# The low parts of all weights on one engine: GpSimd's share of the weight split is given to VectorE

## The chip, the cores and the metric

The kernel runs on one core of one Trainium2 chip. The core has TensorE (PE in the profile), VectorE (DVE), ScalarE (ACT), GpSimd (POOL) and SyncE (SP), which issues the weight transfers. Each engine works through its own queue in order and waits for the others by semaphores. The metric is the device time of one execution in microseconds (us); less is better. Several executions are timed, and their median is given.

## What is computed

Two stacks of transformer layers follow each other on 512 tokens of width 1024, all in float32. Cut to what matters:

```
# first stack, twice:
x = x + 0.5 * rmsnorm(swiglu(rmsnorm(x), w_gate, w_up, w_down))    # ffn1, hidden width 2816
x = x + rmsnorm(token_mixing(rmsnorm(x)))                          # mix1: band, difference and stick-breaking attention
x = x + 0.5 * rmsnorm(swiglu(rmsnorm(x), ...))                     # ffn2
# 16 meta tokens are put in front; second stack, twice:
h = h + rmsnorm(mixer(rmsnorm(h)))                                 # mix2: forgetting attention, a conv of 31 taps, a short conv
h = h + rmsnorm(down(silu(conv3(g)) * conv3(up)))                  # ffn3
```

Every product with a weight, `y @ w`, is computed to about float32 from operands of a reduced format (float32r). A float32 operand is split into a high part, which is its rounding to that format, and a low part, which is what is left. Then `x w` is formed as `xh wh + xl wh + xh wl`, three matmuls for each one of the mathematics.

## The kernel before

**Tiling.** The state lies as eight tiles of 128 channels by 528 tokens (`xT`). Tokens are worked in two halves, of up to 272 columns. A weight comes in units of 128 by up to 1056 values: eight blocks of 128 by 128 side by side. A unit is used by one run of matmuls (`mm3`, lines 222 to 224, or lines 799 to 801 for the value projections).

**The weight stream.** `plan` lists all units in the order of use. `load` (line 183) brings one unit in two pieces: SyncE issues the transfer of a piece into a raw buffer `wr` (four of them), ScalarE rounds it into `wh` (line 200), and the subtraction `wl = wr - wh` follows (line 201). `wh` and `wl` have four buffers each. `wunit` hands out the next unit and calls for those up to three ahead. Which engine does the subtraction is chosen at line 193. Before, it is GpSimd for all units of the mixers (mix1 and mix2) and for the first four units of each block but the first (`HEADS`), and VectorE for all others. A unit has two pieces, so that GpSimd does 292 of the 1068 subtractions: 128 in mix1, 124 in mix2, 40 at the heads of the feed-forward blocks.

**What else VectorE does.** At the boundary between two blocks (`boundary`, line 374 on) it scales the block's result by its norm (line 383), adds it to the state (line 389), forms the low part `xl` of the next operand (line 405), and sums squares (lines 346 and 426). In mix1 it does the running products of the stick-breaking part (lines 991 and 993), softmax parts, low parts of the weights of attention (line 927), and it takes the outputs from the PSUM bank (lines 939, 940, 965). In mix2 it computes two depthwise convolutions of 31 taps (line 1350, 120 instructions in the program), evacuates the projections, and forms the forget gate `lf` (line 1186), which TensorE transposes (line 1211).

**The order.** The program is written as generators that are woven together by estimated step times (`weave`, `pipeline`, `Filler`). Behind that stands a scheduler of the framework, which orders the instructions of each engine by its own estimate of when their operands are there. So a change of one instruction's engine can move others, on all engines.

Below, a "subtraction" is always an instruction of line 201, a "tap" one of line 1350.

Of the kernel before, what the change touches and what calls it, by code (L numbers as in the profile page):

```python
# [79 lines left out]
def block_stack_kernel(ctx: ExitStack, tc: tile.TileContext, x_in, meta_in, vec_in, lam_in, wup1, wdn1, wqk1,  # L80
# [3 lines left out]
    act, dve, pe, pool = nc.scalar, nc.vector, nc.tensor, nc.gpsimd  # L84
# [53 lines left out]
    plan, ready, HEADS = [], {}, set()  # L138
# [26 lines left out]
    def wsrc(key, n, c0):  # L165
        kind, l, name = key[:3]
        if name in ("up", "dn"):
            arr = {"up": (wup1, wup2), "dn": (wdn1, wdn2)}[name][kind == "ffn3"]
            i = l if kind == "ffn3" else 2 * l + (kind == "ffn2")
            return arr[i, key[3], key[4]] if name == "up" else arr[i, key[3], :, c0:c0 + n]  # L170
        arr = {"mix1": {"qk": wqk1, "v": wv1, "wo": wo1},
               "mix2": {"qk": wqk2, "v": wv2, "wo": wo2, "cv": wcv2, "pw": wpw2}}[kind][name]
        ap = arr[l]
        for i in key[3:]:
            ap = ap[i]
        return ap[:, 0:n]
# [8 lines left out]
    def load():  # L185

        i = head[1]
        head[1] += 1
        k, n, c0 = plan[i]
        hi = wp.tile([128, 1056], F32R, tag="wh", bufs=4, name="wh")  # L190
        lo = wp.tile([128, 1056], F32R, tag="wl", bufs=4, name="wl")
        ready[i] = hi, lo
        eng = pool if k[0][:3] == "mix" or i in HEADS else dve
        src = wsrc(k, n, c0)
        m = n // 2 if n == 1056 else (n // 128 + 1) // 2 * 128
        for a, b in ((0, m), (m, n)):
            raw = wp.tile([128, 528], F32, tag="wr", bufs=RAWS, name="wr")
            nc.sync.dma_start(out=raw[:, :b - a], in_=src[:, a:b])
            yield raw
            act.activation(out=hi[:, a:b], in_=raw[:, :b - a], func=ACTF.Copy)  # L200
            eng.tensor_tensor(out=lo[:, a:b], in0=raw[:, :b - a], in1=hi[:, a:b].bitcast(F32), op=ALU.subtract)  # L201

    def fetch(to):
        while head[1] < min(to, len(plan)):
            for _ in load():
                pass
# [37 lines left out]
    class Whole:  # L244

        i, n, g, c = None, TALL - T0, slice(T0, TALL), slice(0, TALL - T0)
# [1378 lines left out]
    g0 = VCOL[pre[k0], l0]  # L1625
    nc.sync.dma_start(out=vec[:, g0:g0 + KC], in_=vec_in[:, g0:g0 + KC])
    u0, u1 = load(), load()
    load_x(0, 0, 2)
    next(u0)
# [170 lines left out]
```

## Time and profile before

| | us |
|---|---|
| timed runs | 3595.52, 3599.58, 3600.26 |
| median | 3599.58 |
| profiled execution | 3593.15 |
| its span, first to last instruction | 3591.3 |
| mean granted TensorE clock | 0.966 of full speed |

The profiled execution lies 6.4 us under the median, and 1.85 us of it lie around the span. The page of the profile gives busy time for each engine, the same in 40 slices, and the costliest groups of instructions. Busy time on TensorE is modelled, since its matmuls overlap. The blocks follow each other in the span about so: ffn1 to 370, mix1 to 683, ffn2 to 1062, ffn1 to 1441, mix1 to 1755, ffn2 to 2134, mix2 to 2458, ffn3 to 2859, mix2 to about 3190, ffn3 to the end. So there are nine boundaries between blocks and two passes through each mixer.

### The profile page before, as it was taken

Reading aid. Unit: us, or ns where it says so; the run is one execution under the profiler, and the core shown is the slowest. Engines: PE = TensorE matmul, PEld = TensorE weight load, DVE = VectorE, ACT = ScalarE, POOL = GpSimd, SP = SyncE. Lnnn points to the kernel's source line nnn. Section 1 sums busy time; section 2 is a strip of 40 time slices with the busy share of each in tenths; the row PEclk is TensorE's granted clock in tenths of the full one; section 3 lists DMA queues with packets and bytes.
Section 4 is the critical chain, followed back from the end, with each engine's and each line's share of the span. In section 5 each row is a group of like instructions: output and inputs, shape, how many; then the busy total and the mean of one; then the engine's idle time right before and its main releaser. Section 6 shows DMA issues by size and latency. Waiting matters only on the chain.

```text
span 3591.3 us, 56445 instructions
## 1 busy us (share of the span) xinstructions
PE 3443.0 (96%) x21851; PEld 3055.9 (85%) x21851; DVE 2025.5 (56%) x4145; ACT 1530.7 (43%) x3335; POOL 439.4 (12%) x439
## 2 busy tenths in 40 slices
PE   9999989999999999989999998989999989899998
PEld 8888877888888888877988888879999988799998
DVE  5442777654335442777644349546774386467753
ACT  5323555533234332555633334555443345554432
POOL 0000322200010000322200014212000132120000
PEclk9999999999999999999999999979999989899999
DMA  4233212132332223222133322102222221023232
GB/s 143 94 94 94 71 56 73 49 106 94 94 91 92 94 90 93 66 61 70 60 100 94 93 90 78 51 30 71 95 94 88 87 75 57 30 62 104 90 92 78
DMA packets 165820, 291.43 MB, mean 81 GB/s; under 512 B 19456, under 2 KB 36896, under 8 KB 165552
## 3 DMA queue, kind: packets, MB, share of 16 engines
q1 hardware_dynamic: 163648, 287.13, 25.7%
q8 instruction: 172, 2.82, 0.3%
q10 hardware_dynamic: 1904, 0.70, 0.1%
q14 instruction: 96, 0.79, 0.1%
HBM read 285.62 MB, written 2.13 MB: 80 GB/s over the span
## 4 chain that ended last, share of the span: by engine, by line
PE 83%; DVE 13%; ACT 2%; issue 1%; DMA 0%; POOLq 0%; SPq 0%; ACTq 0%; DVEq 0%
PE ps_acc L222 9%; PE ps_acc L223 9%; PE ps_acc L224 9%; PE ps_s L222 7%; PE ps_s L223 7%; PE ps_s L224 7%; PE ps_x L223 4%; PE ps_x L222 4%; PE ps_x L224 4%; PE ps_o L222 4%; PE ps_o L223 4%; PE ps_o L224 4%; DVE y L1350 3%; PE ps_o L840 2%; PE ps_s L823 2%
## 5 line engine op out<-in xcount | busy, mean ns | idle before, releaser
L200 ACT ACTIVATE wh<-wr 128x512 fp32r<-128x512 f32 (+2 forms) x1068 | 615.4, 614 | 1105.3 <-PE ps_acc L223 453.5
L201 DVE TENSOR_TENSOR wl<-wr,wh 128x512 fp32r<-128x512 f32 (+1 forms) x776 | 499.3, 670 | 440.6 <-ACT wh L200 429.9
L201 POOL TENSOR_TENSOR wl<-wr,wh 128x512 fp32r<-128x512 f32 (+1 forms) x292 | 408.5, 1421 | 2627.5 <-ACT wh L200 2619.8
L222 PE MATMUL ps_acc<-xh,wh 128*128 128x256 f32 (+2 forms) x1600 | 537.7, 336 | 0.0
L223 PE MATMUL ps_acc<-xl,wh 128*128 128x256 f32 (+2 forms) x1600 | 526.9, 329 | 0.0
L224 PE MATMUL ps_acc<-xh,wl 128*128 128x256 f32 (+2 forms) x1600 | 525.4, 328 | 0.0
L223 PE MATMUL ps_s<-xl,wh 128*128 128x512 f32 (+3 forms) x1088 | 361.5, 332 | 12.8 <-DVE xl L405 12.5
L222 PE MATMUL ps_s<-xh,wh 128*128 128x512 f32 (+3 forms) x1088 | 360.8, 332 | 1.0 <-ACT xh L312 0.7
L224 PE MATMUL ps_s<-xh,wl 128*128 128x512 f32 (+3 forms) x1088 | 359.7, 331 | 0.2 <-DVE wl L201 0.2
L222 PEld LDWEIGHTS ps_acc<-xh,wh 128*128 128x128 f32 x1600 | 311.4, 195 | 28.3 <-issue 2.2
L224 PEld LDWEIGHTS ps_acc<-xh,wl 128*128 128x128 f32 x1600 | 310.6, 194 | 25.0 <-issue 0.2
L223 PEld LDWEIGHTS ps_acc<-xl,wh 128*128 128x128 f32 x1600 | 311.3, 195 | 22.4
L223 PEld LDWEIGHTS ps_s<-xl,wh 128*128 128x128 f32 x1088 | 207.5, 191 | 34.7 <-DVE xl L405 15.1
L222 PEld LDWEIGHTS ps_s<-xh,wh 128*128 128x128 f32 x1088 | 207.9, 191 | 21.8 <-ACT xh L312 1.1
L224 PEld LDWEIGHTS ps_s<-xh,wl 128*128 128x128 f32 x1088 | 207.4, 191 | 19.7 <-DVE wl L201 0.4
L222 PE MATMUL ps_x<-xh,wh 128*128 128x256 f32 (+3 forms) x608 | 206.1, 339 | 0.0
L223 PE MATMUL ps_x<-xl,wh 128*128 128x256 f32 (+3 forms) x608 | 203.9, 335 | 0.0
L224 PE MATMUL ps_x<-xh,wl 128*128 128x256 f32 (+3 forms) x608 | 203.0, 334 | 0.0
L223 PE MATMUL ps_o<-xl,wh 128*128 128x512 f32 (+3 forms) x544 | 179.7, 330 | 5.1 <-DVE xl L405 5.1
L222 PE MATMUL ps_o<-xh,wh 128*128 128x512 f32 (+3 forms) x544 | 179.0, 329 | 0.0
L224 PE MATMUL ps_o<-xh,wl 128*128 128x512 f32 (+3 forms) x544 | 178.7, 328 | 0.0
L223 PE MATMUL ps_acc<-hl,wh 128*128 128x256 f32 (+1 forms) x528 | 168.7, 319 | 0.0
(360 smaller groups left out, 7982.6 us busy)
## 6 DMA issues: line engine op xcount, KB each, us to landing
wr<-in_wup_dram SPq DMA_DIRECT2D x528, 256.0 KB, 2.8
wr<-in_wdn_dram SPq DMA_DIRECT2D x192, 256.0 KB, 2.7
wr<-in_wqk_dram SPq DMA_DIRECT2D x96, 256.0 KB, 2.7
wr<-in_wdn_dram SPq DMA_DIRECT2D x96, 192.0 KB, 2.6
wr<-in_wo_dram SPq DMA_DIRECT2D x64, 256.0 KB, 2.7
wr<-in_wv_dram SPq DMA_DIRECT2D x40, 256.0 KB, 2.6
wr<-in_wcv_dram SPq DMA_DIRECT2D x40, 256.0 KB, 2.6
dec<-fdram SPq DMA_DIRECT2D x16, 264.0 KB, 3.7
```

What stands on the lines that cost most here:

```text
L200: act.activation(out=hi[:, a:b], in_=raw[:, :b - a], func=ACTF.Copy)
L201: eng.tensor_tensor(out=lo[:, a:b], in0=raw[:, :b - a], in1=hi[:, a:b].bitcast(F32), op=ALU.subtract)
L222: pe.matmul(out=o, lhsT=wh[wsl], rhs=xh[xsl], start=start, stop=False)
L223: pe.matmul(out=o, lhsT=wh[wsl], rhs=xl[xsl], start=False, stop=False)
L224: pe.matmul(out=o, lhsT=wl[wsl], rhs=xh[xsl], start=False, stop=stop)
L823: pe.matmul(out=o, lhsT=a[R, qs], rhs=b[R, ks], start=j == 0, stop=j == 2 and mask is None)
L840: pe.matmul(out=o[:, q0:], lhsT=v, rhs=p[j], start=kb == 0 and j == 0, stop=kb == n - 1 and j == 1)
L1350: dve.scalar_tensor_tensor(out=y[:, s:], in0=t[0][:, :TALL - s], scalar=w[:, 30 - s:31 - s], in1=y[:, s:], op0=ALU.mult, op1=ALU.add))
```

## The change

One line of `load` is changed. The subtraction of every piece of every weight is issued on VectorE.

```diff
@@ load(), line 193 @@
-        eng = pool if k[0][:3] == "mix" or i in HEADS else dve
+        eng = dve
```

Nothing else is changed in the source. GpSimd keeps some 150 small instructions (constants, the scaling of `lrow`, half of the last block's additions). The scheduler orders the rest anew from there.

At the boundary from ffn1 to mix1 (span 370 to 390) VectorE's queue held no subtraction before. `xT` is the state, `f` the block's result, `xl` the low part of the next operand. Before:

```order
L358 RECIPROCAL rt<-rt_s 128x2
L360 COPY R<-rt 128x256
L346 TENSOR_TENSOR sqo<-sqo 128x256
L383 TENSOR_TENSOR f<-f,ps_t 128x256 x2
L389 TENSOR_TENSOR xT<-xT,f 128x256
L383 TENSOR_TENSOR f<-f,ps_t 128x256
L389 TENSOR_TENSOR xT<-xT,f 128x256
L383 TENSOR_TENSOR f<-f,ps_t 128x256
L405 SCALAR_TENSOR_TENSOR xl<-xT,vec,xh 128x256
```

After, at the same place:

```order
L358 RECIPROCAL rt<-rt_s 128x2
L360 COPY R<-rt 128x256
L201 TENSOR_TENSOR wl<-wr,wh 128x512
L346 TENSOR_TENSOR sqo<-sqo 128x256
L383 TENSOR_TENSOR f<-f,ps_t 128x256
L201 TENSOR_TENSOR wl<-wr,wh 128x512
L383 TENSOR_TENSOR f<-f,ps_t 128x256
L389 TENSOR_TENSOR xT<-xT,f 128x256
L383 TENSOR_TENSOR f<-f,ps_t 128x256
L389 TENSOR_TENSOR xT<-xT,f 128x256
L383 TENSOR_TENSOR f<-f,ps_t 128x256
L405 SCALAR_TENSOR_TENSOR xl<-xT,vec,xh 128x256
```

Two subtractions stand in the run, four more come before the last of the eight `xl`, and two behind it.

In mix2 the forget gate `lf` (line 1186) stands between taps in VectorE's queue. Before, the rows ahead of it were:

```order
L1350 SCALAR_TENSOR_TENSOR y<-av,vec,y 128x506
L771 SCALAR_TENSOR_TENSOR ql<-qt,qh 128x256
L1350 SCALAR_TENSOR_TENSOR y<-av,vec,y 128x505
L1350 SCALAR_TENSOR_TENSOR y<-av,vec,y 128x527
L1350 SCALAR_TENSOR_TENSOR y<-av,vec,y 128x504
L769 TENSOR_TENSOR qt<-ps_acc,rb 128x272
L1350 SCALAR_TENSOR_TENSOR y<-av,vec,y 128x503
L771 SCALAR_TENSOR_TENSOR ql<-qt,qh 128x272
L1350 SCALAR_TENSOR_TENSOR y<-av,vec,y 128x502
L1350 SCALAR_TENSOR_TENSOR y<-av,vec,y 128x526
L1350 SCALAR_TENSOR_TENSOR y<-av,vec,y 128x501
L1186 SCALAR_TENSOR_TENSOR lf<-lft,lfe 128x40
```

After:

```order
L201 TENSOR_TENSOR wl<-wr,wh 128x512
L1350 SCALAR_TENSOR_TENSOR y<-av,vec,y 128x511
L201 TENSOR_TENSOR wl<-wr,wh 128x512
L1350 SCALAR_TENSOR_TENSOR y<-av,vec,y 128x510
L1346 TENSOR_SCALAR y<-av,vec 128x528
L1350 SCALAR_TENSOR_TENSOR y<-av,vec,y 128x509
L1350 SCALAR_TENSOR_TENSOR y<-av,vec,y 128x527
L1350 SCALAR_TENSOR_TENSOR y<-av,vec,y 128x508
L769 TENSOR_TENSOR qt<-ps_acc,rb 128x272
L1350 SCALAR_TENSOR_TENSOR y<-av,vec,y 128x507
L771 SCALAR_TENSOR_TENSOR ql<-qt,qh 128x272
```

Three taps follow these rows, and then line 1186. Between the first evacuation of the block (line 1338) and line 1186 there were 29 taps and no subtraction; now there are 25 taps and six subtractions (three more stand ahead of that first evacuation, around line 360).

On TensorE the transposes of that gate (line 1211) stood in the middle of the key projection of the first pair of heads. Before:

```order
L222 MATMUL ps_acc<-xh,wh 128x272
L223 MATMUL ps_acc<-xl,wh 128x272
L224 MATMUL ps_acc<-xh,wl 128x272
L1211 MATMUL ps_t<-ident,lf 8x16
L1211 MATMUL ps_t<-ident,lf 8x128 x4
L222 MATMUL ps_acc<-xh,wh 128x272
```

After:

```order
L224 MATMUL ps_acc<-xh,wl 128x256
L823 MATMUL ps_s<-qh 16x16
L823 MATMUL ps_s<-ql,qh 16x16
L823 MATMUL ps_s<-qh,ql 16x16
L827 LDWEIGHTS identb
L827 MATMUL ps_s<-fmask,identb 16x16
L823 MATMUL ps_s<-qh 128x144
L1211 MATMUL ps_t<-ident,lf 8x16
L1211 MATMUL ps_t<-ident,lf 8x128 x4
```

Between the value projection and line 1211 there were 37 triples of lines 222 to 224; now there are 48 triples and the first score products. In the second mix2 it is the same on both engines, with a few more score products.

## Rows read from the trace of the kernel before

**Rows 1.** The page, busy us of each engine, its share and instructions.

```profile
PE 3443.0 (96%) x21851; PEld 3055.9 (85%) x21851; DVE 2025.5 (56%) x4145; ACT 1530.7 (43%) x3335; POOL 439.4 (12%) x439
```

**Rows 2.** Groups by line: busy us, mean ns | idle before, and what ended it.

```profile
L201 DVE TENSOR_TENSOR wl<-wr,wh 128x512 fp32r<-128x512 f32 (+1 forms) x776 | 499.3, 670 | 440.6 <-ACT wh L200 429.9 <-PE ps_s L224 0.2
L201 POOL TENSOR_TENSOR wl<-wr,wh 128x512 fp32r<-128x512 f32 (+1 forms) x292 | 408.5, 1421 | 2627.5 <-ACT wh L200 2619.8 <-DVE f L383 4.3 <-POOL wl L201 1.7
```

**Rows 3.** Stretches: length; busy PE, PEld, DVE, ACT, POOL; PEclk, DMA share, GB/s.

```profile
352.00:412.00 60.00, 53.10 (x422) 52.21 (x422) 40.20 (x86) 28.08 (x68) 16.93 (x12) 0.94 0.21 67
412.00:500.00 88.00, 77.62 (x519) 65.41 (x518) 67.91 (x114) 48.81 (x119) 28.64 (x20) 0.96 0.22 67
500.00:660.00 160.00, 151.25 (x947) 124.38 (x947) 111.60 (x333) 87.63 (x234) 33.66 (x25) 0.94 0.18 55
...
2165.00:2265.00 100.00, 87.16 (x707) 81.21 (x707) 89.84 (x175) 43.83 (x108) 41.12 (x49) 0.95 0.26 80
2265.00:2450.00 185.00, 172.99 (x1165) 149.97 (x1164) 82.08 (x237) 100.84 (x247) 45.66 (x68) 0.87 0.15 45
```

**Rows 4.** The same stretches for line 201 alone: DVE, then POOL busy.

```profile
2165.00:2265.00 100.00, 0.00 (x0) 36.02 (x24) 0.95 0.26 80
2265.00:2450.00 185.00, 0.00 (x0) 39.24 (x30) 0.87 0.15 45
```

**Rows 5.** VectorE's groups by form, and by line for the taps of line 1350.

```profile
L201 DVE TENSOR_TENSOR wl<-wr,wh 128x512 fp32r<-128x512 f32 x680 | 454.0, 687 | 440.6 <-ACT wh L200 429.9 <-PE ps_s L224 0.2
L389 DVE TENSOR_TENSOR xT<-xT,f 128x256 f32<-128x256 f32 x120 | 67.5, 563 | 0.0
L346 DVE TENSOR_TENSOR sqo<-sqo 128x256 f32<-128x256 f32 x119 | 65.8, 567 | 107.0 <-ACT sqo L338 106.5
...
L771 DVE SCALAR_TENSOR_TENSOR ql<-qt,qh 128x256 fp32r<-128x256 f32 x32 | 23.3, 737 | 3.0 <-ACT qh L770 3.0
...
L549 DVE TENSOR_TENSOR hl<-gu,hh 128x256 fp32r<-128x256 f32 x16 | 6.7, 421 | 0.2
...
L568 DVE SCALAR_TENSOR_TENSOR y<-z,vec,y 128x526 f32<-128x526 f32 (+3 forms) x176 | 132.2, 757 | 3.2 <-ACT y L566 0.5
L1350 DVE SCALAR_TENSOR_TENSOR y<-av,vec,y 128x525 f32<-128x525 f32 (+16 forms) x120 | 108.1, 907 | 0.8
```

**Rows 6.** First boundary, in order of time: start, us, engine, line, tiles [idle before].

```profile
374.71 0.41 DVE L389 TENSOR_TENSOR xT<-xT,f 128x256 f32<-128x256 f32 x1
375.78 1.52 DVE L389 TENSOR_TENSOR xT<-xT,f 128x256 f32<-128x256 f32 x1
375.61 2.85 POOL L201 TENSOR_TENSOR wl<-wr,wh 128x512 fp32r<-128x512 f32 x2 [1.43 <-ACT wh L200]
```

**Rows 7.** TensorE's waits, whole span: us in total, times, longest.

```profile
PE ps_o L840 <- DVE yl L940: 24.7, 12, 3.3
PE ps_t L354 <- DVE sqo L346: 24.5, 10, 4.8
PE ps_t L1211 <- DVE lf L1186: 21.4, 2, 10.7
PE ps_s L223 <- DVE xl L405: 12.5, 11, 2.2
PE ps_o L223 <- DVE xl L405: 5.1, 6, 1.5
```

**Rows 8.** First mix2, in order of time: VectorE, GpSimd and TensorE up to line 1211.

```profile
2172.61 0.42 DVE L1338 TENSOR_TENSOR av<-ps_s,rb 128x256 f32<-128x256 f32 x1 [1.01 <-ACT rb L300]
2209.94 4.07 DVE L1350 SCALAR_TENSOR_TENSOR y<-av,vec,y 128x502 f32<-128x502 f32 x3
2213.93 0.19 DVE L1186 SCALAR_TENSOR_TENSOR lf<-lft,lfe 128x40 f32<-128x40 f32 x1
...
2210.07 3.40 POOL L201 TENSOR_TENSOR wl<-wr,wh 128x512 fp32r<-128x512 f32 x2 [3.68 <-ACT wh L200]
...
2203.22 0.29 PE L224 MATMUL ps_acc<-xh,wl 128*128 128x272 f32 x1
2214.17 1.13 PE L1211 MATMUL ps_t<-ident,lf 16*8 16x16 f32 x5 [10.66 <-DVE lf L1186]
```

## What the change was predicted to do

> **What bounds the kernel now.** The page comes first: TensorE is busy for 96% of the span and VectorE for 56%, so TensorE's own work sets most of the time [rows 1]. What an engine beside it can win or lose lies in the 148 us in which TensorE is not busy (3591.3 - 3443.0). The second view is therefore the list of what TensorE waits for: the longest items are all VectorE's, 24.7 us for line 940, 24.5 for 346, 21.4 for 1186, and 12.5 and 5.1 for `xl` [rows 7]. The third is the table by stretch, which says where VectorE is full: 40.2 of 60 us at a boundary, 67.9 of 88 and 111.6 of 160 in the middle of mix1, 89.8 of 100 in the stretch of mix2 that holds the taps, 82.1 of 185 in the rest of mix2 [rows 3]. GpSimd delays TensorE nowhere in the list. So the question is what 292 more instructions do to VectorE just where TensorE waits for it.
>
> **The price of a subtraction.** On GpSimd one takes 1421 ns on average [rows 2]. On VectorE the same 128x512 form takes 687 ns [rows 5]. 292 x 0.687 = 201 us of new work on VectorE.
>
> **What is refunded.** VectorE is slowed while GpSimd subtracts. At the first boundary the addition of line 389 takes 0.41 us at one place and 1.52 us at another, where a pair of GpSimd's subtractions runs [rows 6]. The means show how common that is. An instruction of two 128x256 operands from SBUF takes 421 ns where GpSimd is idle (line 549), but lines 389, 346 and 771 average 563, 567 and 737 [rows 5]: 120 x 0.142 + 119 x 0.146 + 32 x 0.316 = 44.5 us. The taps average 907 ns against 757 for the like instruction of line 568: 120 x 0.15 = 18 us [rows 5]. Taken in this way for every VectorE instruction that overlaps one of GpSimd's (585 of them, of which 190 are slowed by over 0.1 us; line 389 in rows 6 is one), the loss is 152 us. It goes away with GpSimd's subtractions. The load of VectorE thus rises by 201 - 152 = 49 us only, in a kernel in which it idles for 1566.
>
> The Trainium skill ("SBUF — State Buffer", Who interferes with whom) gives the mechanism: a VectorE instruction with two SBUF inputs and a GpSimd instruction that reads SBUF need the same port, and the second of them waits for the whole of the first. The 0.41 and 1.52 us agree. By that rule nothing of the loss stays once GpSimd computes no low part.
>
> **Boundaries, nine of them.** In the first one VectorE runs without a pause from 371.7 to 386.7 us, and TensorE waits for `xl` there. Between those times the refund, instruction by instruction, is 5.8 us (16 that overlap GpSimd, the first a line 346, the 1.52 us of rows 6 among them). Six subtractions now stand in that run. The first falls into an idle 0.9 us, the other five cost 5 x 0.687 = 3.4. The last `xl` comes 2.4 us earlier. TensorE's waits for `xl` are 17.6 us in all, about 2 for each boundary, and those for line 346 are 24.5 [rows 7]; the latter is mostly the way from TensorE through ScalarE to VectorE, which does not change. I take 1.5 us for each boundary, **-14 us** in all. Bounds: -22 (all of the 2.4 at each) and -4 (TensorE has other work where `xl` comes early).
>
> **The taps, twice.** 24 subtractions fall into 2165 to 2265 [rows 4], 24 x 0.687 = 16.5 us; the refund in it is 16.3 us, over 60 instructions. The sum is unchanged at the fullest place of the program. What changes is the order. Before, TensorE reached line 1211 at 2203.5 and stood still for 10.7 us, until line 1186 ended; VectorE had begun its run at 2172.6 and was at it until 2213.9 [rows 8]. In that run the refund is 11.2 us (21 instructions overlap, the last are three taps that take 4.07 in place of some 2.1 [rows 8]), four taps are put behind line 1186 (4 x 0.67 = 2.7 us), and six subtractions come in (4.1). ScalarE now rounds eight pieces ahead of line 300, where it did four, which delays the run by up to 2.3 us. Line 1186 then ends about 7.5 us sooner, near 2206. TensorE has 11 triples and some score products more ahead of line 1211, 39 matmuls or about 4.7 us at 0.12 each, and comes there at 2208. The wait of 10.7 us is gone. But VectorE stays full until about 2262, and TensorE can't run far ahead of it. From line 1186 on VectorE has about nine subtractions and four taps more (6.2 + 2.7) and 4.3 us of refund, so that its backlog ends 7.5 - 4.6 = 3 us sooner. Between 10.7 us kept whole and 0, I take 4 for each pass, near VectorE's own 3, **-8 us** in all (bounds -21 and 0).
>
> Here a rule of the Trainium skill speaks against the change: "Perfetto Trace Analysis", Optimizing Scalar/DVE Operations, holds that work may be offloaded, even to GpSimd, where VectorE is saturated, but adds that the shared port may spoil it. By its first half the 24 subtractions would lengthen this stretch by 16.5 us at each pass; the refund of rows 5 and 6 bears out the second half.
>
> **The middle of mix1, twice.** 20 subtractions in 412 to 500 (GpSimd runs nothing else there [rows 3]) and 24 in 500 to 660 cost 13.7 + 16.5 us; the refunds are 9.3 and 7.6, since much of VectorE's work here reads PSUM and isn't slowed. VectorE gets 13.3 us more in 248. TensorE is idle for 10.4 and 8.8 us of these [rows 3], mostly for lines 940 and 965. Where it is busy, later work of VectorE costs nothing until the next wait. I take a fifth, 2.5 us, twice: **+5 us** (bounds 0 and +27, all of it on the path).
>
> **The rest of mix2, twice.** 30 subtractions [rows 4], 20.6 us, refund 5.7; VectorE gets 14.9 us more, but it is busy for only 82 of 185 [rows 3]. A tenth, twice: **+3 us** (bounds 0 and +30).
>
> **What costs nothing.** In the feed-forward bodies nothing moves. The subtractions wait for ScalarE's `wh`, as GpSimd's did; in the queue they stand where, by the trace of before, `wh` is ready in nearly all places of mix1 and the boundaries, so VectorE doesn't stand still for them. A later subtraction would free its raw buffer later; the units are brought up to three ahead, which hides a delay of one or two us. If that cover were gone, TensorE would wait for `wh` or `wl`, which it hardly does now.
>
> **Sum.** -14 - 8 + 5 + 3 = -14 us. The profiled execution, 3593.15 us, becomes 3579. It lies 6.4 us under the median of the three runs; for the median, 3599.58 - 14 = 3585.6, and I write 3585.
>
> **Rivals.** (a) **More is kept.** The wait at line 1211 goes and isn't given back, and the boundaries give their 2.4: -21 - 22 = -43, **3556**. For it: TensorE was busy without a break after 2214, so it wasn't behind VectorE there. Against it: VectorE is full until 2262. (b) **The waits move, and it is even.** VectorE's sum in the full stretches is the same, each wait that goes returns at the next evacuation: -7 to +7, about **3599**. (c) **Slower: the middles of the mixers.** There the refund covers only 44% of the new work (22.6 of 50.8 us for a pass through both). The surplus, 28.2 us, twice, is 56 us at most. Beside boundaries of -14 and taps of -8 it decides from 40% on: if 22 of the 56 reach TensorE, the gain is gone. With two fifths on the path and the boundaries at -4 and no gain at the taps: +23 - 4 = +19, **3618**. For it: VectorE is 77% full in 412 to 500, and TensorE waits 24.7 us for line 940 over the program. Against it: TensorE idles for only 9 us of the 160 that follow, and many subtractions stand at places where VectorE was idle. (d) **No refund.** If the slowing had another cause than GpSimd, the taps alone would cost 2 x 16.5 = 33 us, less 5 of reordering, **3628**. Rows 6 speak against it. That the subtractions stay on GpSimd is no case: in the order all 1068 stand on VectorE.
>
> **Chances.** A measurement of this kernel can tell about 0.2%, 7 us, from no change. The forecast, with (a) as its far end: 0.55 for faster by more than that. (b): 0.25. (c): 0.17, (d): 0.03. Faster 0.55, same 0.25, slower 0.20. The range 3556 to 3618 reaches from (a) to (c) and leaves out (d) and some of what the new order may do that no row shows; the likeliest case alone has 3556 to 3592.
>
> **What would show it.** Right: lines 389, 346 and 771 at 128x256 fall to about 0.42 us and the taps to about 0.75; `xl` waits at boundaries shrink; TensorE's wait at line 1211 is under 3 us. Wrong: those means stay, or the waits for lines 940 and 965 in mix1 grow by more than 5 us a pass, or TensorE waits for `wl`. The first would kill the refund, the second make (c) true, the third show the raw buffers coming free too late.

## The result, and the profile after

| | before, us | after, us |
|---|---|---|
| median of the timed runs | 3598.71 | 3504.44 |
| their range | 3595.52 to 3600.26 | 3498.62 to 3509.24 |
| profiled execution, its span | 3593.15, 3591.3 | 3498.62, 3496.8 |

The ratio is 0.9738, with a 95% interval of 0.9721 to 0.9756. The kernel is 94 us faster, where 14 had been predicted, and the time lies far below the range of 3556 to 3618.

The page after the change, busy time and instructions of each engine, and the shares of the chain of work that ended last:

```profile
PE 3415.8 (98%) x21851; PEld 3025.0 (87%) x21851; DVE 2039.6 (58%) x4437; ACT 1528.4 (44%) x3335; POOL 29.4 (1%) x147
...
PE 88%; DVE 8%; ACT 2%; issue 1%; DMA 0%; SPq 0%; POOLq 0%; ACTq 0%; DVEq 0%
```

Against [rows 1], VectorE has 292 instructions more and is busy for only 14 us more. TensorE is idle for 81 us of the span in place of 148. Its busy time fell as well, by 27 us, at a mean granted clock of 0.981 in place of 0.966. So 67 + 27 = 94 us.

VectorE's groups after, by form (line 1350 over all its forms): busy us, mean ns | idle before, and what ended it.

```profile
L201 DVE TENSOR_TENSOR wl<-wr,wh 128x512 fp32r<-128x512 f32 x960 | 641.5, 686 | 480.9 <-ACT wh L200 469.1 <-PE ps_s L224 0.2
L389 DVE TENSOR_TENSOR xT<-xT,f 128x256 f32<-128x256 f32 x120 | 50.1, 418 | 0.0
L346 DVE TENSOR_TENSOR sqo<-sqo 128x256 f32<-128x256 f32 x119 | 48.4, 421 | 68.2 <-ACT sqo L338 67.9
...
L1350 DVE SCALAR_TENSOR_TENSOR y<-av,vec,y 128x525 f32<-128x525 f32 (+17 forms) x120 | 87.6, 740 | 0.3
...
L771 DVE SCALAR_TENSOR_TENSOR ql<-qt,qh 128x256 fp32r<-128x256 f32 x32 | 12.9, 418 | 1.7 <-ACT qh L770 1.5
```

The slowing is gone: lines 389, 346 and 771 take 418, 421 and 418 ns where [rows 5] had 563, 567 and 737, the taps 740 where they took 907, and the subtraction costs the same 686 ns as before. Summed over all records, VectorE's subtractions rose by 199 us and everything else on it fell by 153. (The page's 14 is less than 199 - 153 = 46, because it counts overlapping records once. Back to back, a subtraction takes 0.60 us from start to start.)

What TensorE waits for after: us in total, times, longest.

```profile
PE ps_acc L222 <- DVE qt L769: 16.6, 3, 7.8
PE ps_o L840 <- DVE yl L940: 15.6, 12, 2.6
PE ps_o L840 <- DVE y L1295: 4.1, 4, 1.2
...
PE ps_o L840 <- DVE yb L965: 3.6, 6, 0.9
...
PE ps_t L1079 <- DVE bR L1077: 1.4, 2, 0.7
PE ps_t L1211 <- DVE lf L1186: 1.3, 1, 1.3
...
PE ps_t L354 <- DVE sqo L346: 0.9, 1, 0.9
```

Against [rows 7]: the waits for line 346 (24.5) and for `xl` (17.6) are gone, line 940 has fallen from 24.7 to 15.6, and line 1186 from 21.4 to 1.3. Two waits are new, both in mix2: 16.6 us for line 769, the evacuation of a projection, and 4.1 for line 1295. Three waits of before that [rows 7] leaves out belong to the sum too:

```profile
PE ps_o L840 <- DVE yb L965: 7.1, 6, 2.2
...
PE ps_t L354 <- DVE sq L426: 5.0, 3, 2.4
PE ps_t L1079 <- DVE bR L1077: 5.0, 6, 1.2
```

With them the 67 us of idle time can be laid out: boundaries (lines 346, 426, `xl`) 47.1 to 0.9, so **-46**; mix1 (lines 940, 965, 1077) 36.8 to 20.6, so **-16**; the gate of mix2 with the new waits for lines 769 and 1295, 21.4 to 22.0, so **about 0**. That makes 62 of the 67; the rest is spread over short waits.

**The first boundary.** Columns of the stretch: length; busy PE, PEld, DVE, ACT, POOL; clock, DMA share, GB/s. Before:

```profile
378.00:390.00 12.00, 7.46 (x49) 6.89 (x48) 11.74 (x23) 7.72 (x20) 6.08 (x5) 0.81 0.34 116
```

After:

```profile
378.00:390.00 12.00, 12.00 (x103) 11.98 (x102) 11.43 (x31) 6.24 (x17) 0.00 (x0) 1.00 0.41 131
```

VectorE is as full after as before, 11.4 of 12 us. But TensorE gets 103 matmuls through in place of 49. Before, it stood still three times, as its timeline shows (start, us, [idle before <- what ended it]):

```profile
380.14 0.28 PE L222 MATMUL ps_s<-xh,wh 128*128 128x256 f32 x1
381.08 0.39 PE L223 MATMUL ps_s<-xl,wh 128*128 128x256 f32 x1 [0.66 <-DVE xl L405]
...
384.97 0.39 PE L223 MATMUL ps_s<-xl,wh 128*128 128x256 f32 x1 [2.21 <-DVE xl L405]
...
387.25 0.99 PE L354 MATMUL ps_t<-onec,sqo 128*128 128x1 f32 x4 [1.67 <-DVE sqo L346]
388.10 0.56 PE L223 MATMUL ps_acc<-xl,wh 128*128 128x256 f32 x1
388.46 0.41 PE L224 MATMUL ps_acc<-xh,wl 128*128 128x256 f32 x1
```

That is 4.5 us, and behind it the matmuls ran at half the granted clock (0.50 of full speed in 386 to 392; 0.41 us for one in place of 0.28, and 0.56 for the first). After, at the same place:

```profile
382.51 0.28 PE L222 MATMUL ps_s<-xh,wh 128*128 128x256 f32 x1
382.63 0.28 PE L222 MATMUL ps_acc<-xh,wh 128*128 128x256 f32 x1
382.75 0.28 PE L222 MATMUL ps_s<-xh,wh 128*128 128x256 f32 x1
382.88 0.28 PE L223 MATMUL ps_s<-xl,wh 128*128 128x256 f32 x1
...
385.67 0.58 PE L354 MATMUL ps_t<-onec,sqo 128*128 128x1 f32 x4
```

No wait is left. The new order also draws products of the high part (line 222) ahead of those that need `xl`.

### The profile page after: what moved, and what is told of

Same layout as the page of the kernel before. It is cut to its first block, busy times and chain, and to the rows that moved or that the text cites. A ratio compares the mean times of both kernels' runs of the same rounds, so it can differ in the third digit from the quotient of the medians.

```text
span 3496.8 us, 56301 instructions
## 1 busy us (share of the span) xinstructions
PE 3415.8 (98%) x21851; PEld 3025.0 (87%) x21851; DVE 2039.6 (58%) x4437; ACT 1528.4 (44%) x3335; POOL 29.4 (1%) x147
## 4 chain that ended last, share of the span: by engine, by line
PE 88%; DVE 8%; ACT 2%; issue 1%; DMA 0%; SPq 0%; POOLq 0%; ACTq 0%; DVEq 0%
PE ps_acc L222 10%; PE ps_acc L224 10%; PE ps_acc L223 10%; PE ps_s L223 8%; PE ps_s L222 8%; PE ps_s L224 8%; PE ps_x L222 4%; PE ps_x L223 4%; PE ps_x L224 4%; PE ps_o L223 4%; PE ps_o L222 4%; PE ps_o L224 4%; PE ps_o L840 2%; PE ps_s L823 2%; DVE wl L201 1%
## 5 line engine op out<-in xcount | busy, mean ns | idle before, releaser
L201 DVE TENSOR_TENSOR wl<-wr,wh 128x512 fp32r<-128x512 f32 (+2 forms) x1068 | 693.8, 673 | 480.9 <-ACT wh L200 469.1
L222 PE MATMUL ps_acc<-xh,wh 128*128 128x256 f32 (+2 forms) x1600 | 531.9, 332 | 16.6 <-DVE qt L769 16.6
L224 PE MATMUL ps_acc<-hh,wl 128*128 128x256 f32 (+1 forms) x528 | 168.3, 319 | 0.0
```

Of the source, the lines that this page charges most:

```text
L222: pe.matmul(out=o, lhsT=wh[wsl], rhs=xh[xsl], start=start, stop=False)
L224: pe.matmul(out=o, lhsT=wl[wsl], rhs=xh[xsl], start=False, stop=stop)
```

## The experiments

Theory P says that the gain is VectorE's lost time on TensorE's path, and that the new work lands mostly where it costs little. Rivals: O (the new order of instructions), L (the load on VectorE decides), and others that came up on the way.

**The old order without the slowing.** GpSimd keeps its instructions but only writes:

```diff
-            eng.tensor_tensor(out=lo[:, a:b], in0=raw[:, :b - a], in1=hi[:, a:b]..., op=ALU.subtract)
+            pool.memset(lo[:, a:b]..., 1e-4) if eng is pool else eng.tensor_tensor(...)
```

> GpSimd fills the low parts of the 292 pieces with a constant (it writes, and reads nothing) where it subtracted before; these low parts are left out of the result. VectorE gets no subtraction. On TensorE, VectorE and SyncE the order of instructions is row by row that of the kernel before. Theory P (path): of the time that VectorE lost to GpSimd's subtractions, 115 us lay on the chain of the kernel before, and that is what the change gives back. Then the old order without that loss gives about 3599 - 115 = 3484 (3465 to 3505), at or below the changed kernel's 3504, and lines 389, 346 and 771 at 128x256 take about 0.42 us. Theory O (order): the gain comes from the new order that the scheduler makes. Then this kernel, with the old order, stays within 20 us of 3599.

Measured: 3453.67 us, ratio 0.9608 (0.9593 to 0.9622). The page, and two groups by form:

```profile
PE 3387.6 (98%) x21851; PEld 3009.1 (87%) x21851; DVE 1876.6 (54%) x4145; ACT 1527.6 (44%) x3335; POOL 176.8 (5%) x439
```

```profile
L201 POOL MEMSET wl<- 128x512 f32 x280 | 139.3, 529 | 2705.5 <-PE ps_x L224 1205.7 <-PE ps_acc L224 1043.9 <-PE ps_o L224 159.0
...
L389 DVE TENSOR_TENSOR xT<-xT,f 128x256 f32<-128x256 f32 x120 | 50.1, 417 | 0.0
```

With before's order on TensorE and VectorE the time falls by 143 us, more than P had said. VectorE is busy for 149 us less. So the slowing alone cost before 143 us, nearly all of it on TensorE's path, and O falls. (That the low parts come sooner here, since a fill is shorter and waits for no `wh`, isn't what was gained: before, TensorE waited for `wl` for 0.2 us in all.) TensorE's waits in that kernel show that the wait at line 1211 was backlog from the slowing too: it isn't in the list at all, with line 1186 at its old place.

```profile
PE ps_o L840 <- DVE yl L940: 12.6, 12, 2.0
PE ps_o L840 <- DVE yb L965: 3.8, 6, 0.8
...
PE ps_t L354 <- DVE sqo L346: 1.3, 3, 0.9
PE ps_acc L222 <- DVE qt L769: 1.2, 3, 0.7
```

**The new work taken away, and doubled.** In one kernel no engine forms the 292 low parts; in the other VectorE forms each of them twice:

```diff
-        eng = dve
+        eng = None if k[0][:3] == "mix" or i in HEADS else dve      # and hi in place of lo
```

> No engine subtracts the 292 pieces: the high part is used in the place of the low one, so that the low parts are left out of the result. TensorE has the same number of matmuls. This gives what the subtractions on VectorE still cost in the changed kernel. P: about the 34 us that they have on its chain, 3460 to 3490. L: 80 us or more, under 3430.

```diff
+            also and dve.tensor_tensor(out=lo[:, a:b], ...same...)      # also: mixers and HEADS
```

> The changed kernel, but VectorE does each of the 292 subtractions twice, so that it gets 201 us more of work and no loss to GpSimd. P: the first 201 us stand on the chain of the changed kernel with 34 us only; as much again costs 30 to 60, 3535 to 3565. Theory L (load, that of my prediction): in the full stretches of mix2 and the middles of the mixers each us on VectorE counts for a fifth to all, and there is no refund to set against it: 80 to 150 more, 3585 to 3655.

Measured: 3456.79 us, ratio 0.9613 (0.9599 to 0.9628), and 3595.03 us, ratio 1.0002 (0.9992 to 1.0012). Their pages:

```profile
PE 3396.8 (98%) x21851; PEld 3018.2 (87%) x21851; DVE 1875.4 (54%) x4145; ACT 1527.8 (44%) x3335; POOL 31.4 (1%) x147
```

```profile
PE 3458.7 (96%) x21851; PEld 3055.2 (85%) x21851; DVE 2203.0 (61%) x4729; ACT 1530.8 (43%) x3335; POOL 30.1 (1%) x147
```

The 292 subtractions cost 48 us in the changed kernel (P had 34, L over 80), a second time 91 (P had 30 to 60, L 80 to 150). P priced both too low, L the first too high; of the second, 91 lies near the lower end of L. The price rises with the load. The order itself is worth little: without the 292 low parts the new order takes 3456.79 us, and the old one, with GpSimd only writing, 3453.67. The balance of the change is -143 + 48 = -95, and the measured one -94.

**The slowing put back on the changed kernel.** VectorE subtracts, and GpSimd repeats each of the 292 into the raw buffer:

```diff
+            also and pool.tensor_tensor(out=raw[:, :b - a], in0=raw[:, :b - a], in1=hi[:, a:b]..., op=ALU.subtract)
```

> The changed kernel, but GpSimd subtracts each of the 292 pieces once more, into the raw buffer, behind VectorE's subtraction. VectorE, TensorE and ScalarE stand in nearly the order of the changed kernel (173 lines of difference of 20867 rows on TensorE). P: the loss is back, on top of the subtractions on VectorE: 3504 + 115 or so, 3590 to 3650. O: the order is the new one, so that it stays at 3500 to 3530.

Measured: 3665.43 us, ratio 1.0192 (1.0177 to 1.0207), 161 us over the changed kernel.

```profile
PE 3475.8 (95%) x21851; PEld 3068.3 (84%) x21851; DVE 2233.8 (61%) x4437; ACT 1532.4 (42%) x3335; POOL 482.3 (13%) x439
```

```profile
L201 DVE TENSOR_TENSOR wl<-wr,wh 128x512 fp32r<-128x512 f32 x960 | 683.5, 731 | 480.8 <-ACT wh L200 470.1 <-PE ps_s L224 0.2
...
L389 DVE TENSOR_TENSOR xT<-xT,f 128x256 f32<-128x256 f32 x120 | 63.5, 529 | 0.0
```

Line 389 is back at 529 ns, and now VectorE's own subtractions are slowed too (731). GpSimd holds the raw buffers longer here, but TensorE waits for `wh` and `wl` for 2.0 us in all (lines 200 and 201), so that is not where the 161 us come from.

**Parts of the change.** Line 193 with one half of its condition:

```diff
+        eng = pool if k[0][:3] == "mix" else dve                      # heads moved
+        eng = pool if i in HEADS and k[0][:3] != "mix" else dve       # mixers moved
```

> Only the 40 subtractions at the heads of the feed-forward blocks are on VectorE; GpSimd keeps the mixers' 252. Theory P (what counts is VectorE's lost time on TensorE's path, place by place, so the parts add up): the feed-forward blocks with the boundaries into the mixers took 23 us of the 94 in the changed kernel; of these the boundaries into the mixers hold mixer units, which stay here. About 15 to 25 us under the kernel before, 3572 to 3585. Theory C (the gain comes as a whole, since TensorE's granted clock rises only when most stalls are gone): under 8 us, 3589 or more, at a clock of 0.966 to 0.968.

> Only the mixers' 252 subtractions are on VectorE; GpSimd keeps the 40 at the heads of the feed-forward blocks. P: 70 to 80 us under the kernel before, 3517 to 3530, and with the other half alone the two gains add up to 94 within 12 us. C: clearly less than its share, 3535 to 3560, and the two gains add up to under 75 us. In both the passes of mix1 are as short as in the changed kernel, 290 us from boundary to boundary.

Measured: 3561.69 us, ratio 0.9905 (0.9888 to 0.9921), and 3533.77 us, ratio 0.9828 (0.9813 to 0.9843). The gains are 35 and 63 us, 97 together against 94: they add up, and theory C falls. The split is not P's: the 40 at the heads give more than was expected, 35 us for a seventh of the instructions, and the mixers less. Both passes of mix1 are as short as in the changed kernel (291 us), as expected.

**One input in place of two.** GpSimd copies `wh` into `wl`:

```diff
+            pool.tensor_copy(out=lo[:, a:b], in_=hi[:, a:b]...) if eng is pool else eng.tensor_tensor(...)
```

> GpSimd keeps its 292 instructions, but each copies the high part (one input from SBUF) and subtracts nothing, so that the low parts of these units are left out and the high parts stand in their place. The order on TensorE, VectorE and SyncE is that of the kernel before. Theory R (whatever GpSimd reads from SBUF holds up VectorE's instructions of two SBUF inputs; only writing does not): line 389 stays well over 0.45 us, VectorE's busy time falls by less than the 149 us of the write-only run in about the proportion in which a copy is shorter than 1.42 us, and the time lies between 3500 and 3590. Theory T (it takes two inputs on GpSimd's side too): line 389 at 0.417, VectorE 1877 us, 3450 to 3462 as in the write-only run.

Measured: 3478.27 us, ratio 0.9674 (0.966 to 0.9688). Groups by form:

```profile
L201 POOL CAST wl<-wh 128x512 fp32r<-128x512 f32 x280 | 195.5, 715 | 2649.4 <-ACT wh L200 2642.4 <-DVE xT L389 3.2 <-DVE f L383 2.0
L389 DVE TENSOR_TENSOR xT<-xT,f 128x256 f32<-128x256 f32 x120 | 55.7, 464 | 0.0
```

Reading one input slows VectorE too (464 against 417), so T falls. The Trainium skill ("SBUF — State Buffer", Who interferes with whom) says that a VectorE instruction with two SBUF inputs contends with a GpSimd instruction that reads SBUF and not with one that only writes. This run and the one that only writes agree. R's size was missed: the copy is half as long as the subtraction, but VectorE's busy time (1909.6) keeps only 33 us of the 149, and the time lies under R's 3500. The timelines show why so little is left. An instruction of GpSimd and a line 389 that begins while it runs, before and then with the copy (start, us):

```profile
379.05 1.29 POOL L201 TENSOR_TENSOR wl<-wr,wh 128x512 fp32r<-128x512 f32 x1 [0.60 <-ACT wh L200]
379.32 1.30 DVE L389 TENSOR_TENSOR xT<-xT,f 128x256 f32<-128x256 f32 x1
```

```profile
378.60 0.62 POOL L201 CAST wl<-wh 128x512 fp32r<-128x512 f32 x1 [0.39 <-ACT wh L200]
378.73 0.76 DVE L389 TENSOR_TENSOR xT<-xT,f 128x256 f32<-128x256 f32 x1
```

VectorE's addition ends 0.28 and 0.27 us behind GpSimd's instruction: it has waited for the rest of that instruction, whether it reads one input or two. A shorter instruction is met less often, and less of it is left when it is met. VectorE has the same order in both kernels and in the one that only writes; compared with that one row by row, 187 of its instructions are over 0.1 us longer before, by 0.80 us on average, and 122 with the copies, by 0.29. That makes 150 and 35 us. R had reckoned with the length alone.

**Is it the place?** Lines 405 and 771, which GpSimd had slowed, are issued twice, on the changed kernel and on the one without the 292 subtractions:

```diff
+            for _ in range(2): dve.scalar_tensor_tensor(out=xl[:, hn.g], ...)
+            for _ in range(2): dve.scalar_tensor_tensor(out=ql[:, h.g], ...)
```

> The changed kernel with the instructions of lines 405 and 771 issued twice, 144 and 72 more; the second writes the same again, and nothing is left out. That is 144 x 0.482 + 72 x 0.511 = 106 us more on VectorE, at two of the lines that GpSimd had slowed, without any GpSimd work. Theory W (what counts is where the time falls: in an instruction whose result TensorE is about to need, an added us costs nearly a us): 80 to 110 us over the changed kernel, 3585 to 3615. Theory S (an added instruction is cheap wherever it stands, since the scheduler knows of it and arranges the rest; only the slowing, of which it doesn't know, is dear): at the price of the subtractions, a quarter to a half, 26 to 50 us, 3530 to 3555.

> The kernel in which nobody computes the 292 low parts (they are left out, the high parts stand in their place), with the instructions of lines 405 and 771 issued twice: 106 us more on VectorE than that kernel's 3457, at two of the lines that GpSimd slows, and no GpSimd work. From the same floor GpSimd's slowing of 148 us had cost 143. Theory W (place: these lines are dear in themselves): 85 to 105 us over the floor, 3542 to 3562. Theory M (an added instruction is priced by how full VectorE already is; the same 106 us cost 59 above the changed kernel): clearly less from the floor, 25 to 45 us, 3482 to 3502. Between, at 50 to 65 us, 3507 to 3522: place decides a part, and what is left to the slowing's own price is that the order of the engines doesn't allow for it.

Measured: 3563.75 us, ratio 0.9905 (0.9885 to 0.9924), and 3492.76 us, ratio 0.9713 (0.9697 to 0.9729). The first lies between W and S, the second is M's: 59 and 36 us. So work at these lines is dearer than a subtraction elsewhere, but it is not as dear as the slowing.

**A cheaper subtraction.** One for each unit in place of two:

```diff
+        raw = wp.tile([128, 1056], F32, tag="wr", bufs=RAWS // 2, name="wr")
         for a, b in ((0, m), (m, n)):      # transfer and rounding in two pieces, as before
+        eng.tensor_tensor(out=lo[:, :n], in0=raw[:, :n], in1=hi[:, :n]..., op=ALU.subtract)
```

> The changed kernel with one subtraction for each unit in place of two (raw buffers of 1056 in place of 528 values, two in place of four), nothing left out. By line 201's rows (0.686 us for 512 values, 0.551 for 384) the fixed part of one is about 0.146 us; 534 instructions fewer are 78 us less on VectorE, 21 us of it in the mixers and at the heads. At the price of the subtractions, a quarter to a half, 5 to 10 us under the changed kernel, 3494 to 3500, if the later release of the raw buffers is hidden. If it is not, TensorE waits for line 200 or 201 and the kernel is slower than the changed one, 3510 to 3550.

Measured: 3480.44 us (3472.30 to 3483.61), ratio 0.9672 (0.9656 to 0.9688). It beats both kernels. Two groups by form:

```profile
L201 DVE TENSOR_TENSOR wl<-wr,wh 128x1024 fp32r<-128x1024 f32 x432 | 527.2, 1221 | 155.8 <-ACT wh L200 155.3
...
L201 DVE TENSOR_TENSOR wl<-wr,wh 128x896 fp32r<-128x896 f32 x96 | 104.8, 1092 | 295.3 <-ACT wh L200 295.3
```

1221 ns in place of 2 x 686 is 0.15 us less for each unit, as expected. But two in a row overlap, so that VectorE's busy time falls by 32 us only (2039.6 to 2007.2) and not by the 78 that the durations add up to. The gain, 24 us by the medians and 15 by the spans, is larger than the 5 to 10 that the mixers' part was priced at; why is not shown. TensorE still doesn't wait for the weights to speak of (2.4 us at line 224), so the later release of the raw buffers is hidden.

**What a microsecond on VectorE costs**, by the pages (busy time) and the medians:

| step | VectorE busy | time | for 1 us |
|---|---|---|---|
| GpSimd copies (against only writing) | +33.0 | +24.6 | 0.75 |
| GpSimd subtracts (before, against only writing) | +148.9 | +143.4 | 0.96 |
| GpSimd repeats the subtractions (on the changed kernel) | +194.2 | +161.0 | 0.83 |
| 292 subtractions put on VectorE | +164.2 | +47.7 | 0.29 |
| the same once more | +163.4 | +90.6 | 0.55 |
| lines 405 and 771 twice, without the 292 | +83.3 | +36.0 | 0.43 |
| the same, on the changed kernel | +84.8 | +59.3 | 0.70 |

From an equal start, slowing costs 0.75 to 0.96, an issued instruction 0.29 to 0.43. From the changed kernel it is 0.83 against 0.55 to 0.70. Two causes are in reach: instructions that are in the program are arranged around by the scheduler (the rows of line 222 above), and the slowing falls just where weights, and with them GpSimd's work, become ready. No run here parts the two, so that stays open. The medians of the kernel before, timed anew beside each group of runs, lie between 3595.56 and 3598.71 us, so that differences between groups carry some 3 us of uncertainty.

## Why the prediction was wrong

**VectorE's account was right.** 201 us of new work and 152 of refund were predicted, 199 and 153 came, and lines 389, 346, 771 and the taps fell to the durations named. The direction follows from that and held.

**The boundaries, -14, were the step that failed most: -46 in idle time alone.** Two readings went wrong there. The 24.5 us for line 346 in [rows 7] were put down to "the way from TensorE through ScalarE to VectorE, which does not change". They came from VectorE's slowed queue: the wait of 1.67 us above ended with a line 346 that stood behind slowed instructions. VectorE before, in order of time:

```profile
382.34 1.17 DVE L389 TENSOR_TENSOR xT<-xT,f 128x256 f32<-128x256 f32 x1
383.43 1.88 DVE L405 SCALAR_TENSOR_TENSOR xl<-xT,vec,xh 128x256 fp32r<-128x256 f32 x2
...
385.90 0.87 DVE L405 SCALAR_TENSOR_TENSOR xl<-xT,vec,xh 128x256 fp32r<-128x256 f32 x2
386.69 0.41 DVE L346 TENSOR_TENSOR sqo<-sqo 128x256 f32<-128x256 f32 x1
```

Line 346 itself takes 0.41 us, without any idle time ahead of it. It waited its turn behind a 1.17 and a 1.88 (against 0.42 and 0.88 after), and with the slowing gone, in either order, TensorE waits for line 346 for 0.9 to 1.3 us in the whole program. In nine of the ten waits VectorE came to line 346 without idle time, when its operand had been ready for 0.3 to 2.4 us, 13.8 us in all. In the longest (4.8 us) it had been ready for only 0.3, since ScalarE's square came late; but ScalarE itself had stood still for line 389 twice, for 2.2 and 0.8 us, so VectorE's queue was behind that as well. And the `xl` waits were valued by how much sooner the last `xl` comes, though TensorE stood still for earlier ones as well. The lower bound of -22 had both errors in it.

**The middle of mix1, +5: -16.** The surplus of work was read correctly, and the two passes show it (columns as above), the first pass before, then after:

```profile
400.30:712.70 312.40, 286.56 (x1926) 246.57 (x1925) 223.78 (x540) 174.85 (x446) 89.67 (x64) 0.95 0.21 63
```

```profile
398.20:688.90 290.70, 279.18 (x1922) 240.41 (x1922) 229.44 (x604) 174.10 (x445) 0.00 (x0) 0.98 0.22 68
```

And where GpSimd only writes:

```profile
393.80:679.60 285.80, 275.46 (x1923) 237.50 (x1922) 194.89 (x540) 174.36 (x446) 31.84 (x64) 0.98 0.22 69
```

VectorE is busy for 5.7 us more, and the pass with its closing boundary is 21.7 us shorter. By the third row the slowing had cost 26.6 us there, and the new work takes 4.9 of them back. The step netted refund against new work inside a stretch and gave both the same price. A us refunded and a us added aren't worth the same here: 0.96 and 0.29.

**The taps, -8, and the rest of mix2, +3.** The wait at line 1211 went, as predicted, and most of it came back at the next evacuation, as predicted: line 769 now holds TensorE for 16.6 of the 21.4 us of both passes, line 1295 for another 4.1. Net nothing, where -8 was taken; rival (b) had this place right. The +3 can't be read apart. The first pass of mix2, with its boundary, went from 327.9 to 316.1 us, and takes 303.1 where GpSimd only writes: the slowing had cost 24.8 us, and the new work takes 13.0 of them back, more than in mix1.

**TensorE's busy time wasn't in the sum.** The prediction said that what can be won lies in the 148 us in which TensorE isn't busy. 27 of the 94 us lay outside: with fewer stops the granted clock rose, and the same 21851 matmuls took less time.

**The rivals.** (a) had the right sign and stopped at 43, for it rested on the same reading of the boundaries. (b) described the return of the waits rightly, but for the taps alone. (c) would have needed longer waits for lines 940 and 965; both fell. (d) falls with the durations. The third sign of a miss that was named, TensorE waiting for `wl`, didn't come either (0.2 us). The rule that work may go to GpSimd where VectorE is saturated (the Trainium skill, "Perfetto Trace Analysis", Optimizing Scalar/DVE Operations) had to be read with its own reservation on the shared port: here the work on GpSimd cost 143 us and the same work on VectorE 48.

## What to carry to other kernels

A helper engine that shares a port doesn't cost what it does, but what it holds up: look for one instruction form with two durations, sum the excess, and price that excess at nearly its full size (0.75 to 0.96 here) if the slowed engine feeds the bound one. Price work that moves in separately, and don't net the two inside a stretch. A wait that ends with a short instruction can be a wait for the whole queue in front of it: follow that queue back before calling the wait fixed.

## What the runs showed of the hardware

GpSimd's instructions that only write left VectorE unslowed (417 ns for line 389, with GpSimd busy for 177 us), those that read one input slowed it a little (464), those that read two, and take twice as long, slowed it much (563). In both the slowed instruction waited to the end of GpSimd's: in the 76 cases before, and the 57 with the copies, in which an instruction of 0.42 us was slowed so, it ended 0.27 to 0.29 us behind it. Line 769, which takes one of its inputs from PSUM, began 14 times while GpSimd subtracted and was not lengthened once. VectorE's short instructions overlap in the records: a 0.69 us subtraction is followed by the next instruction's start after 0.60. And the granted clock went with the stops: in the 12 us of the first boundary it was 0.81 with 4.5 us of standing still and 1.00 without, so that a stop costs more than its own length.
